# One step of a hybrid diffusion backbone: more weight parts made by transfers, and the attention placed anew

## The chip, the core and the metric

The kernel runs on one core of a Trainium2 chip. The metric is device time in microseconds (us) of one launch; lower is better. In the profile PE is TensorE, PEld its weight load, DVE VectorE, ACT ScalarE, POOL GpSimd, and SP the engine that issues most of the DMAs.

## The reference

One trunk layer, D = 2048, two request groups of 128 tokens each (context tokens and latent tokens), all in fp32:

```python
m = silu(c) @ w_ada + b_ada                       # shift, scale, gate, twice
h = rms_norm(x) * (1 + scale1) + shift1
qA, kA, vA, qB, kB, vB, gA, gB = split(h @ w_in)  # 2048 x 8704
oA = windowed GQA with sink, QK-norm, rotary      # 8 heads, 2 key heads, cached context
oB = 2-D neighbourhood attention with bias        # 8 heads, cached context
x  = x + gate1 * ((sigmoid(gA) * (oA @ w_br_a) + sigmoid(gB) * (oB @ w_br_b)) @ w_out)
h2 = rms_norm(x) * (1 + scale2) + shift2
x  = x + gate2 * (relu(h2 @ w_up) ** 2 @ w_down)  # 2048 x 8192 and back
```

The outputs are both groups' `x` and the new context keys and values.

## The kernel before

The weights are read once, in 456 steps of 128 x 1024 fp32 (512 KB). Steps 0 to 135 are `w_in` (the projections up to step 85, then the gates gB, gA), 136 to 167 the two branch projections, 168 to 199 `w_out`, and 200 to 455 the MLP: `w_up` in eight pieces p, with `w_down` interleaved.

TensorE multiplies in fp32r, which is narrower than fp32, so every weight is split in two: a high part `wH` (fp32r copy of the loaded `raw`, ScalarE, line 103) and a low part `wL` = `raw` - `wH` (VectorE, line 269). A product then takes three matmuls: high times high, low times high, high times low. A plain step has 12 matmuls of 128 x 512. In the pieces 1 to 7 of `w_up` some pairs of steps (`FAST`, by position) run a Strassen-like scheme instead: x (6 matmuls) and y (15), whose operands `XH`, `XL`, `YB`, `tH`, `tL`, `uH`, `uL` ScalarE and VectorE make (lines 1299 to 1325); slow pairs have 24.

Where the parts come from is set by three lists. A step in `LO_DMA` has its low part made by `minus_plus`: ScalarE writes -`wH` (line 275), and an accumulating DMA on GpSimd's queue adds the weight once more from memory (line 276). `XL_DMA` does the same for the `XL` of a fast pair (index 8 p + position). A step in `HI_DMA` has its high part loaded by a casting DMA on GpSimd's queue (line 239); if it is in `LO_DMA` as well, there is no `raw`, no copy and no subtraction. In the kernel before `HI_DMA` is empty.

All these tiles share one pool of 50 buffers. Each engine works its instructions off in the order in which the program emits them. That order is written out by hand in tables: `run()` walks the steps; `RUN[i]` tells how many steps ahead of step i (beyond `LOAD` = 4) the loads are emitted, `LOOK[i]` how many steps ahead the parts are made, and low parts by transfer two steps (`LO_AHEAD`) before that. `DOTS` places the dot products of the gate and modulation vectors (line 1476, VectorE, a tile each, one dot per request group) among the steps. `POST` gives for each projection unit the steps at which its squares are taken, its norm is applied, and it is transposed; `JOBS` the steps of the attention's stages.

VectorE also does the softmax reductions, ScalarE the squares (753), the norm's application (764), exponentials (866, 872), gates (671), and the evacuations of transposes (103, 800). TensorE transposes (794, 888) and multiplies (895).

Of the kernel before, what the change touches and what calls it, by code (L numbers as in the profile page):

```python
# [31 lines left out]
LOAD = 4  # L32
FB_DVE = 2
FB1 = 10
H_AT = 2
FILL = {1: [("gB", 2), ("gB", 3)], 3: [("gB", 0), ("gB", 1)]}
DOTS1 = [9, 11, 14, 19, 22, 24, 25, 27, 28, 30, 32, 33, 34, 35, 37, 40, 41, 42, 44, 46, 48, 49, 51, 53]
CHUNKS = [2, 2, 2, 4, 6]
NFAST = 8
FAST = {1: (0, 2, 5, 7), 2: (0, 4, 5, 6, 7), 3: (0, 2, 4, 5, 7), 4: (0, 2, 4, 5, 7), 5: (0, 1, 3, 4, 7), 6: (0, 3, 4, 5, 7), 7: (0, 1, 3, 6, 7)}  # L40
SEED_AT = 3
QK_ACT = [('qB', 1)]
H2_DVE = [(0, 1), (0, 3), (1, 1), (1, 3)]
KEEP = True
ROWS_AT = [8, 11, 7]
SEED1_AT = 2
SEED1 = "111110100100111111011111111011011111"
BACK = 9
AWAY = [('gA', 1), ('gB', 2), ('gB', 3), ('gA', 0), ('gB', 0), ('gA', 2)]
GATE_BACK = 2  # L50
DIRECT = (3,)
LO_DMA = [50, 54, 56, 63, 77, 107, 129, 141, 145, 176, 184, 188, 189, 203, 228, 233, 250, 286, 297, 360, 388, 392, 403, 447]
LO_AHEAD = 2

LOOK = "610013015100121312024402233324102425654224523344556654121016645555652437464478554443414661516353316110022636320000411134313543044023400458230315565645456443574337324421522555644666784051000205311111322534111433455554321045445111013410444324654734331001335565775443654453304436533423355423455542233213213545587654334232213213202440122544412433432313432443523324313211333435533333213331314344422557756822145342656433332302254541454475574464555546763333345544"
RUN = "345110004667224234111350007998421004464200022565595544354324444434399864356664356543323535443144230021224242014401314415432457530331035587986564665545676867644543555342013141147676676965699967265287998988511453877787785653022200123446553345324545104653232464345673321110102122521121211202355533232133432223443232410110000000011234344212022112531112752123301000112323643331133410100122454235566436675432012021222210010001154457832224556577677636445664422134"
CONST_AT = [83, 79]
XL_DMA = [8]
HI_DMA = []
ADA_AT = [None, 4, 13, 22, 25]  # L60
XS_AT = {1: 3, 2: 25, 3: 34}
POST = {('kvA', 0): [81, 83, 89], ('qA', 0): [84, 86, 92], ('qA', 1): [86, 88, 92], ('kB', 0): [90, 94, 98], ('qB', 0): [94, 98, 104], ('kB', 1): [98, 101, 103], ('qB', 1): [102, 105, 107]}
JOBS = [[93, 94, 95, 100, 106], [93, 94, 98, 104, 106], [98, 98, 100, 106, 114], [101, 104, 107, 110, 111], [107, 107, 110, 115, 120], [109, 109, 111, 118, 121], [113, 114, 115, 126, 128], [116, 116, 119, 122, 124]]
SS_AT = [120, 127]
T_AT = [4, 4]
PREP_IN = [5, 7]
DOTS = [44, 58, 61, 61, 62, 63, 65, 66, 66, 66, 69, 70, 71, 71, 72, 74, 76, 81, 84, 85, 89, 91, 94, 96, 96, 96, 100, 100, 101, 102, 102, 105, 107, 107, 107, 110, 110, 111, 113, 114, 115, 117, 117, 117, 120, 120, 120, 121, 121, 123, 123, 124, 127, 128, 128, 132, 132, 133, 133, 134, 135, 136, 141, 143, 144, 144, 149, 151, 151, 152, 157, 157, 157, 162, 163, 170, 172, 174, 174, 174, 176, 176, 178, 182, 183, 187, 190, 190]
# [13 lines left out]
def tile_hybrid_step(ctx: ExitStack, tc: tile.TileContext, a):  # L81
# [148 lines left out]
    def add_step(src, mm, key, half=0):  # L230
# [59 lines left out]

    by_dma = sorted(LO_DMA)

    def run():
        loads.sort(key=lambda x: x[:2])
        for st in wsteps:
            while loads and loads[0][0] <= st["i"] + int(RUN[st["i"]]):
                loads.pop(0)[2]()
            for j in sorted(j for j in pre if j <= st["i"]):
                for fn in pre.pop(j):
                    fn()  # L300
            to = st["i"] + int(LOOK[st["i"]]) + 1
            while by_dma and by_dma[0] < to + LO_AHEAD:
# [945 lines left out]
    def up_pair(p):  # L1248
        n0, n1 = PIECES[p]
        w, box, key = a["w_up"], {"begun": set()}, ("up", n0)  # L1250
        fast = FAST[p]

# [28 lines left out]
        for pos, is_fast in enumerate(kinds):  # L1281
# [90 lines left out]
            for i, (nm, pf, mf) in enumerate((("x", prep_x, mm_x), ("y", prep_y, mm_y))):  # L1372
# [284 lines left out]
```

## Time and profile before

| | |
|---|---|
| median of 3 runs | 1315.7 us (1315.65 to 1315.85) |
| the profiled execution | 1315.82 us |
| its span | 1314.0 us |
| TensorE busy | 1300.4 us, 99% |
| VectorE busy | 1147.5 us, 87% |
| ScalarE busy | 918.2 us, 70% |
| GpSimd busy | 61.3 us, 5% |
| HBM over the span | 291 GB/s |
| granted clock | 1.00 throughout (the upper of the two levels, 2.4 GHz) |

The span runs from the first instruction to the last; 1.8 us of the execution lie outside it. The shares of busy time are averages over stages with different limits, so the stages are read one by one in the rows further down.

### The profile page before, as it was taken

How to read it: one execution, taken by the hardware profiler on the slowest of the kernel's cores; microseconds unless marked ns; L12 is line 12 of the kernel's file. 1: busy time of each engine (PE TensorE's matmuls, PEld its weight loads, DVE VectorE, ACT ScalarE, POOL GpSimd, SP SyncE). 2: the span in 40 equal slices, each digit the busy share in tenths (PEclk: the TensorE clock that was granted, in tenths of full speed). 3: DMA queues.
4: the chain of work that ended last, by engine and by line, in shares of the span. 5: the costliest groups of instructions: out<-in, count | busy, mean ns of one | idle time of the engine just before them, and what ended most of it. 6: DMA issues, size and time to landing. Idle time of an engine off the chain costs nothing.

```text
span 1314.0 us, 17445 instructions
## 1 busy us (share of the span) xinstructions
PE 1300.4 (99%) x5978; PEld 1051.5 (80%) x5978; DVE 1147.5 (87%) x1531; ACT 918.2 (70%) x1299; POOL 61.3 (5%) x67
## 2 busy tenths in 40 slices
PE   8999999999999999999999999999999999999998
PEld 4677888888777788888888888888888888888886
DVE  4578999999899999999879998897989998979753
ACT  5656766689865655745687867869678687796881
POOL 0000000332100000000000000000000000000000
PEclk9999999999999999999999999999999999999999
DMA  9999999898889999999398775888586697867692
GB/s 373 408 406 410 378 362 323 317 325 296 287 344 388 401 387 315 372 356 375 107 335 300 261 250 173 279 292 280 199 299 230 211 317 250 295 160 304 197 349 80
DMA packets 148313, 393.80 MB, mean 300 GB/s; under 512 B 51680, under 2 KB 52672, under 8 KB 148224
## 3 DMA queue, kind: packets, MB, share of 16 engines
q1 hardware_dynamic: 144064, 378.18, 78.7%
q0 software_dynamic: 4016, 14.42, 5.7%
q8 instruction: 47, 0.77, 0.2%
q14 instruction: 42, 0.34, 0.1%
q10 hardware_dynamic: 144, 0.08, 0.0%
HBM read 373.97 MB, written 8.70 MB: 291 GB/s over the span
## 4 chain that ended last, share of the span: by engine, by line
PE 68%; DVE 4%; DMA 2%; ACT 2%; issue 1%; ACTq 0%; DVEq 0%; SPq 0%
PE acc L321 14%; PE acc L322 14%; PE acc L320 14%; PE Q L1259 6%; PE Q L1260 6%; PE Q L1258 6%; DVE aT L1476 1%; DVE wL L269 1%; DMA raw<-in_w_br_a 1%; DVE junk L1476 1%; DMA g_gA<-gm_gA 1%; PE Z L1259 1%; PE Z L1260 1%; PE Z L1258 1%; DMA gm_gA<-g_gA 1%
## 5 line engine op out<-in xcount | busy, mean ns | idle before, releaser
L269 DVE TENSOR_TENSOR wL<-raw,wH 128x1024 fp32r<-128x1024 f32 x361 | 425.8, 1224 | 63.6 <-ACT wH L103 62.8
L103 ACT ACTIVATE wH<-raw 128x1024 fp32r<-128x1024 f32 (+1 forms) x391 | 387.7, 1043 | 62.3 <-PE acc L321 9.6
L1476 DVE SCALAR_TENSOR_TENSOR aT<-aT,cB 128x1024 f32<-128x1024 f32 x144 | 173.9, 1224 | 1.1
L1476 DVE SCALAR_TENSOR_TENSOR junk<-aT,cB 128x1024 bf16<-128x1024 f32 x144 | 173.9, 1224 | 0.0
L451 PE MATMUL acc<-wH,hH 128*128 128x512 f32 x276 | 108.4, 393 | 0.7 <-ACT acc L103 0.7
L452 PE MATMUL acc<-wL,hH 128*128 128x512 f32 x276 | 107.5, 389 | 0.0
L453 PE MATMUL acc<-wH,hL 128*128 128x512 f32 x276 | 107.4, 389 | 0.0
L103 ACT ACTIVATE uH<-raw 128x1024 fp32r<-128x1024 f32 x34 | 36.1, 1063 | 65.4 <-DVE raw L1322 59.8
L451 PEld LDWEIGHTS acc<-wH,hH 128*128 128x128 f32 x276 | 51.8, 188 | 15.0 <-issue 2.5
L453 PEld LDWEIGHTS acc<-wH,hL 128*128 128x128 f32 x276 | 51.8, 188 | 11.0
L452 PEld LDWEIGHTS acc<-wL,hH 128*128 128x128 f32 x276 | 51.8, 188 | 10.4
L103 ACT ACTIVATE tH<-t 128x1024 fp32r<-128x1024 f32 x34 | 36.0, 1058 | 28.7 <-DVE t L1315 27.7
L320 PE MATMUL acc<-wH,hH 128*128 128x512 f32 x128 | 52.3, 408 | 0.0
L321 PE MATMUL acc<-wL,hH 128*128 128x512 f32 x128 | 50.2, 392 | 0.6 <-DVE wL L269 0.6
L486 PE MATMUL acc<-wH,hH 128*128 128x512 f32 x128 | 50.4, 393 | 0.0
L487 PE MATMUL acc<-wL,hH 128*128 128x512 f32 x128 | 50.0, 390 | 0.2 <-DVE wL L269 0.2
L322 PE MATMUL acc<-wH,hL 128*128 128x512 f32 x128 | 50.0, 391 | 0.0
L488 PE MATMUL acc<-wH,hL 128*128 128x512 f32 x128 | 49.9, 390 | 0.0
L1325 DVE TENSOR_TENSOR uL<-raw,uH 128x1024 fp32r<-128x1024 f32 x34 | 41.7, 1225 | 1.1
L1315 DVE TENSOR_TENSOR t<-raw 128x1024 f32<-128x1024 f32 x34 | 41.4, 1219 | 1.3 <-PE Q L1259 1.3
L1324 DVE TENSOR_TENSOR tL<-t,tH 128x1024 fp32r<-128x1024 f32 x34 | 41.4, 1219 | 0.0
L103 ACT ACTIVATE acc<-dsum 128x512 f32<-128x512 f32 x56 | 31.7, 589 | 13.8 <-DVE up L1360 7.1
(649 smaller groups left out, 3337.7 us busy)
## 6 DMA issues: line engine op xcount, KB each, us to landing
raw<-in_w_in SPq DMA_DIRECT2D x133, 512.0 KB, 8.0
raw<-in_w_down SPq DMA_DIRECT2D x128, 512.0 KB, 5.8
aT<-in_w_adaT SPq DMA_DIRECT2D x80, 512.0 KB, 8.3
raw<-in_w_upF SPq DMA_DIRECT2D x68, 512.0 KB, 5.5
aT<-in_w_gT SPq DMA_DIRECT2D x64, 512.0 KB, 6.8
raw<-in_w_up SPq DMA_DIRECT2D x60, 512.0 KB, 6.1
araw<-in_w_pair SPq DMA_DIRECT2D x48, 512.0 KB, 9.6
raw<-in_w_out SPq DMA_DIRECT2D x32, 512.0 KB, 10.0
```

Source lines behind the costliest of these rows:

```text
L103: act.activation(out, in_, AF.Copy)
L269: dve.tensor_tensor(st["lo"], st["raw"], st["hi"].bitcast(F32), op=OP.subtract)
L320: pe.matmul(acc[tb], sh, wh[:, k, :], start=f, stop=False, skip_group_check=seeded)
L321: pe.matmul(acc[tb], sh, wl[:, k, :], start=False, stop=False, skip_group_check=seeded)
L322: pe.matmul(acc[tb], sl, wh[:, k, :], start=False, stop=l, skip_group_check=seeded)
L451: pe.matmul(acc[tb], sh, wh[:, k, :], start=opened[u] and k == 0, stop=False, skip_group_check=skip)
L452: pe.matmul(acc[tb], sh, wl[:, k, :], start=False, stop=False, skip_group_check=skip)
L453: pe.matmul(acc[tb], sl, wh[:, k, :], start=False, stop=last and k == 1, skip_group_check=skip)
L1258: pe.matmul(acc, stat[0], hi, start=f, stop=False)
L1259: pe.matmul(acc, stat[0], lo, start=False, stop=False)
L1260: pe.matmul(acc, stat[1], hi, start=False, stop=l)
L1476: dve.scalar_tensor_tensor(out, box["raw"], 1.0, cB[s, tag], op0=OP.mult, op1=OP.mult, accum_out=dst[:, s, fb:fb + 1])
```

## The change

Only tables change. `HI_DMA` gets 26 steps of the MLP, 21 of which are in `LO_DMA` too, all of them new there; the other five (270, 272, 276, 336, 340) still load `raw`. In `LO_DMA` 144 stands for 141 as well. `XL_DMA` gets five fast pairs, of pieces 2 and 4, and in those two pieces `FAST` has other positions. `RUN` and `LOOK` change in 29 and 14 places, between steps 54 and 125; the attention's tables change by one to two steps; one `DOTS` entry goes from 61 to 58. Instruction counts stay on TensorE and ScalarE (26 copies to `wH` become 26 negating copies), VectorE has 26 subtractions fewer, GpSimd's queue 52 DMAs more, SP's 21 fewer.

```diff
-H_AT = 2
+H_AT = 3
...
-FAST = {1: (0, 2, 5, 7), 2: (0, 4, 5, 6, 7), 3: (0, 2, 4, 5, 7), 4: (0, 2, 4, 5, 7), 5: (0, 1, 3, 4, 7), 6: (0, 3, 4, 5, 7), 7: (0, 1, 3, 6, 7)}
+FAST = {1: (0, 2, 5, 7), 2: (0, 3, 4, 6, 7), 3: (0, 2, 4, 5, 7), 4: (0, 4, 5, 6, 7), 5: (0, 1, 3, 4, 7), 6: (0, 3, 4, 5, 7), 7: (0, 1, 3, 6, 7)}
...
-SEED1 = "111110100100111111011111111011011111"
+SEED1 = "111110100100111111011111111001011111"
...
-GATE_BACK = 2
+GATE_BACK = 1
...
-LO_DMA = [50, 54, 56, 63, 77, 107, 129, 141, 145, 176, 184, 188, 189, 203, 228, 233, 250, 286, 297, 360, 388, 392, 403, 447]
+LO_DMA = [50, 54, 56, 63, 77, 107, 129, 144, 145, 176, 184, 188, 189, 203, 223, 228, 233, 234, 237, 243, 250, 266, 286, 297, 306, 308, 341, 349, 357, 360, 373, 381, 388, 389, 392, 403, 425, 430, 436, 440, 442, 446, 447, 451, 453]
...
-XL_DMA = [8]
-HI_DMA = []
+XL_DMA = [8, 19, 20, 22, 36, 38]
+HI_DMA = [223, 234, 237, 243, 266, 270, 272, 276, 306, 308, 336, 340, 341, 349, 357, 373, 381, 389, 425, 430, 436, 440, 442, 446, 451, 453]
...
-POST = {('kvA', 0): [81, 83, 89], ('qA', 0): [84, 86, 92], ('qA', 1): [86, 88, 92], ('kB', 0): [90, 94, 98], ('qB', 0): [94, 98, 104], ('kB', 1): [98, 101, 103], ('qB', 1): [102, 105, 107]}
+POST = {('kvA', 0): [81, 83, 89], ('qA', 0): [84, 86, 92], ('qA', 1): [84, 86, 90], ('kB', 0): [88, 92, 96], ('qB', 0): [94, 98, 104], ('kB', 1): [98, 101, 103], ('qB', 1): [102, 106, 107]}
...
-SS_AT = [120, 127]
+SS_AT = [118, 127]
...
-STAT_AT = [-1, -1, 8, 15]
+STAT_AT = [-2, -1, 8, 17]
...
-M_AT = [6, 6, 9]
+M_AT = [4, 6, 9]
```

Of `JOBS` one normalisation goes from step 98 to 99, one transpose from 106 to 105.

The first place is GpSimd's queue from the first fast pair of the MLP on (piece 1 of `w_up`), before:

```order
L276 DMA XL<-in_w_upF 128x1024
L276 DMA wL<-in_w_up 128x1024
L276 DMA wL<-in_w_down 128x1024
L276 DMA wL<-in_w_up 128x1024 x2
L276 DMA wL<-in_w_down 128x1024 x2
L276 DMA wL<-in_w_up 128x1024
L276 DMA wL<-in_w_down 128x1024 x3
```

and now, up to the high part of step 276 (the rows before reach to the end of the kernel):

```order
L276 DMA XL<-in_w_upF 128x1024
L239 DMA wH<-in_w_up 128x1024
L276 DMA wL<-in_w_up 128x1024 x2
L239 DMA wH<-in_w_down 128x1024 x2
L276 DMA wL<-in_w_down 128x1024 x3
L239 DMA wH<-in_w_down 128x1024
L276 DMA wL<-in_w_down 128x1024
L276 DMA wL<-in_w_up 128x1024
L276 DMA XL<-in_w_upF 128x1024 x3
L239 DMA wH<-in_w_down 128x1024
L276 DMA wL<-in_w_down 128x1024
L239 DMA wH<-in_w_down 128x1024 x3
```

Casting loads (line 239) and accumulations (line 276) now alternate in one in-order queue.

The second is ScalarE's queue at piece 2 of `w_up`, steps 251 to 260, before:

```order
L103 ACTIVATE wH<-raw 128x1024 x5
L103 ACTIVATE XH<-raw 128x1024
L103 ACTIVATE YB<-raw 128x512
L103 ACTIVATE tH<-t_7225 128x1024
L103 ACTIVATE uH<-raw 128x1024
L103 ACTIVATE XH<-raw 128x1024
L103 ACTIVATE YB<-raw 128x512
L103 ACTIVATE tH<-t_7244 128x1024
L103 ACTIVATE uH<-raw 128x1024
L103 ACTIVATE XH<-raw 128x1024
```

and now:

```order
L103 ACTIVATE wH<-raw 128x1024 x3
L103 ACTIVATE XH<-raw 128x1024
L275 ACTIVATE XL<-XH 128x1024
L103 ACTIVATE YB<-raw 128x512
L103 ACTIVATE tH<-t_7189 128x1024
L103 ACTIVATE uH<-raw 128x1024
L103 ACTIVATE XH<-raw 128x1024
L275 ACTIVATE XL<-XH 128x1024
L103 ACTIVATE YB<-raw 128x512
L103 ACTIVATE tH<-t_7235 128x1024
L103 ACTIVATE uH<-raw 128x1024
L103 ACTIVATE wH<-raw 128x1024 x2
```

Steps 254 and 255 have become a fast pair; the second `XH` is that of step 256, which before was the first. Each of the two is followed by its negating copy.

The third is VectorE's queue at steps 56 to 62, where `junk` and `aT` are the two dots of a tile, before:

```order
L107 TENSOR_TENSOR hL_1828<-xnT_79,hH_1827 128x512
L269 TENSOR_TENSOR wL<-raw,wH 128x1024 x2
L1476 SCALAR_TENSOR_TENSOR junk,gc_g_361<-aT,cB_1115 128x1024
L269 TENSOR_TENSOR wL<-raw,wH 128x1024 x5
L1476 SCALAR_TENSOR_TENSOR aT,gc_g_361<-aT,cB_1117 128x1024
L269 TENSOR_TENSOR wL<-raw,wH 128x1024
L1476 SCALAR_TENSOR_TENSOR junk,gc_g_361<-aT,cB_1115 128x1024 x2
```

and now:

```order
L107 TENSOR_TENSOR hL_1830<-xnT_79,hH_1829 128x512
L269 TENSOR_TENSOR wL<-raw,wH 128x1024 x2
L1476 SCALAR_TENSOR_TENSOR junk,gc_g_361<-aT,cB_1115 128x1024 x2
L269 TENSOR_TENSOR wL<-raw,wH 128x1024 x5
L1476 SCALAR_TENSOR_TENSOR aT,gc_g_361<-aT,cB_1117 128x1024 x2
L269 TENSOR_TENSOR wL<-raw,wH 128x1024
L1476 SCALAR_TENSOR_TENSOR junk,gc_g_361<-aT,cB_1115 128x1024
```

One dot pair has moved ahead: its first dot stands before the five `wL` of steps 60 to 65 rather than behind them.

## Rows read from the trace of the kernel before

**Rows 1.** Windows: PE, PEld, DVE, ACT, POOL busy us (count), clock, DMA share, GB/s.

```profile
400.00:450.00 50.00, 49.97 (x266) 39.21 (x266) 49.97 (x79) 28.32 (x36) 0.86 (x1) 1.00 1.03 395
700.00:750.00 50.00, 50.00 (x222) 41.42 (x221) 48.75 (x62) 39.98 (x40) 0.86 (x1) 1.00 0.95 328
1200.00:1250.00 50.00, 50.00 (x223) 41.40 (x222) 38.43 (x40) 36.20 (x43) 0.00 (x0) 1.00 0.67 216
```

**Rows 2.** Waits of TensorE, 250 to 480 us: releaser, us in total, times, longest.

```profile
PE ps_PT L888 <- ACT T_qB L800: 0.9, 1, 0.9
PE acc L321 <- DVE wL L269: 0.8, 2, 0.6
PE ps_o L895 <- ACT probT L103: 0.8, 1, 0.8
PE acc L451 <- ACT acc L103: 0.7, 1, 0.7
PE ps_qT L794 <- ACT T_kB L103: 0.4, 1, 0.4
PE ps_qT L794 <- DVE oLA L904: 0.4, 1, 0.4
PE ps_gr L1497 <- DVE gc_g L1482: 0.2, 1, 0.2
```

**Rows 3.** Waits of VectorE, 204 to 475 us, the largest.

```profile
DVE wL L269 <- ACT wH L103: 3.6, 3, 2.8
```

**Rows 4.** Timeline, VectorE at step 61: start, duration, engine, line, instruction, [idle before].

```profile
203.64 1.23 DVE L269 TENSOR_TENSOR wL<-raw,wH 128x1024 fp32r<-128x1024 f32 x1 [0.25 <-ACT wH L103]
```

**Rows 5.** Timelines of ScalarE, TensorE and VectorE at five places of the attention.

```profile
259.32 1.06 ACT L103 ACTIVATE wH<-raw 128x1024 fp32r<-128x1024 f32 x1 [1.47 <-DVE aT L1476]
...
260.92 0.50 PE L451 MATMUL acc<-wH,hH 128*128 128x512 f32 x1 [0.70 <-ACT acc L103]
...
336.55 0.40 PE L321 MATMUL acc<-wL,hH 128*128 128x512 f32 x1
...
338.27 1.22 DVE L269 TENSOR_TENSOR wL<-raw,wH 128x1024 fp32r<-128x1024 f32 x1
...
347.36 1.23 DVE L269 TENSOR_TENSOR wL<-raw,wH 128x1024 fp32r<-128x1024 f32 x1 [2.85 <-ACT wH L103]
```

**Rows 6.** Accumulating DMAs: all; the one at 755.6; plain loads (KB, us to landing).

```profile
L276 POOL DMA_DIRECT2D wL<-in_w_down x6: 861/863/866, 708.7 to 1270.7; - x6
DMA to landing us min/median/max: 5.3/8.7/10.4
...
L276 POOL DMA_DIRECT2D wL<-in_w_up x1: 857/857/857, 755.6 to 755.6; - x1
DMA to landing us min/median/max: 5.3/5.3/5.3
...
raw<-in_w_down SPq DMA_DIRECT2D x128, 512.0 KB, 5.8
```

**Rows 7.** Timelines, first operand of the fast pair at step 256.

```profile
768.83 1.05 ACT L103 ACTIVATE XH<-raw 128x1024 fp32r<-128x1024 f32 x1
...
771.42 1.22 DVE L1315 TENSOR_TENSOR t<-raw 128x1024 f32<-128x1024 f32 x1
...
784.70 0.39 PE L1259 MATMUL Q<-XL,h20H 128*128 128x512 f32 x1
```

**Rows 8.** Timelines, step 389 and its neighbours.

```profile
1108.68 1.23 DVE L1325 TENSOR_TENSOR uL<-raw,uH 128x1024 fp32r<-128x1024 f32 x1
...
1117.09 1.04 ACT L103 ACTIVATE XH<-raw 128x1024 fp32r<-128x1024 f32 x1
...
1131.01 0.39 PE L1259 MATMUL Q<-wL,h23H 128*128 128x512 f32 x1
```

**Rows 9.** DMA queues: packets, MB, share of 16 engines' span.

```profile
q1 hardware_dynamic: 144064, 378.18, 78.7%
q0 software_dynamic: 4016, 14.42, 5.7%
```

More of the change, by code (lines that the diff above doesn't have):

```diff
@@ L53 @@
 LO_AHEAD = 2
-LOOK = "610013015100121312024402233324102425654224523344556654121016645555652437464478554443414661516353316110022636320000411134313543044023400458230315565645456443574337324421522555644666784051000205311111322534111433455554321045445111013410444324654734331001335565775443654453304436533423355423455542233213213545587654334232213213202440122544412433432313432443523324313211333435533333213331314344422557756822145342656433332302254541454475574464555546763333345544"
-RUN = "345110004667224234111350007998421004464200022565595544354324444434399864356664356543323535443144230021224242014401314415432457530331035587986564665545676867644543555342013141147676676965699967265287998988511453877787785653022200123446553345324545104653232464345673321110102122521121211202355533232133432223443232410110000000011234344212022112531112752123301000112323643331133410100122454235566436675432012021222210010001154457832224556577677636445664422134"
+LOOK = "610013015100121312024402233324102425654224523344556654121016645565652437574377445343414661516353205210022636320000411134313643044023400458230315565645456443574337324421522555644666784051000205311111322534111433455554321045445111013410444324654734331001335565775443654453304436533423355423455542233213213545587654334232213213202440122544412433432313432443523324313211333435533333213331314344422557756822145342656433332302254541454475574464555546763333345544"
@@ L57 @@
+RUN = "345110004667224234111350007998421004464200022565595544243214333434399864346555377654224635443144230021224242114401324405201346530331035587986564665545676867644543555342013141147676676965699967265287998988511453877787785653022200123446553345324545104653232464345673321110102122521121211202355533232133432223443232410110000000011234344212022112531112752123301000112323643331133410100122454235566436675432012021222210010001154457832224556577677636445664422134"
 CONST_AT = [83, 79]
-XL_DMA = [8]
@@ L59 @@
-HI_DMA = []
+XL_DMA = [8, 19, 20, 22, 36, 38]
+HI_DMA = [223, 234, 237, 243, 266, 270, 272, 276, 306, 308, 336, 340, 341, 349, 357, 373, 381, 389, 425, 430, 436, 440, 442, 446, 451, 453]
 ADA_AT = [None, 4, 13, 22, 25]
 XS_AT = {1: 3, 2: 25, 3: 34}
-POST = {('kvA', 0): [81, 83, 89], ('qA', 0): [84, 86, 92], ('qA', 1): [86, 88, 92], ('kB', 0): [90, 94, 98], ('qB', 0): [94, 98, 104], ('kB', 1): [98, 101, 103], ('qB', 1): [102, 105, 107]}
-JOBS = [[93, 94, 95, 100, 106], [93, 94, 98, 104, 106], [98, 98, 100, 106, 114], [101, 104, 107, 110, 111], [107, 107, 110, 115, 120], [109, 109, 111, 118, 121], [113, 114, 115, 126, 128], [116, 116, 119, 122, 124]]
@@ L64 @@
-SS_AT = [120, 127]
+POST = {('kvA', 0): [81, 83, 89], ('qA', 0): [84, 86, 92], ('qA', 1): [84, 86, 90], ('kB', 0): [88, 92, 96], ('qB', 0): [94, 98, 104], ('kB', 1): [98, 101, 103], ('qB', 1): [102, 106, 107]}
+JOBS = [[93, 94, 95, 100, 106], [93, 94, 99, 104, 106], [98, 98, 100, 105, 114], [101, 104, 107, 110, 111], [107, 107, 110, 115, 120], [109, 109, 111, 118, 121], [113, 114, 115, 126, 128], [116, 116, 119, 122, 124]]
+SS_AT = [118, 127]
 T_AT = [4, 4]
 PREP_IN = [5, 7]
-DOTS = [44, 58, 61, 61, 62, 63, 65, 66, 66, 66, 69, 70, 71, 71, 72, 74, 76, 81, 84, 85, 89, 91, 94, 96, 96, 96, 100, 100, 101, 102, 102, 105, 107, 107, 107, 110, 110, 111, 113, 114, 115, 117, 117, 117, 120, 120, 120, 121, 121, 123, 123, 124, 127, 128, 128, 132, 132, 133, 133, 134, 135, 136, 141, 143, 144, 144, 149, 151, 151, 152, 157, 157, 157, 162, 163, 170, 172, 174, 174, 174, 176, 176, 178, 182, 183, 187, 190, 190]
+DOTS = [44, 58, 58, 61, 62, 63, 65, 66, 66, 66, 69, 70, 71, 71, 72, 74, 76, 81, 84, 85, 89, 91, 94, 96, 96, 96, 100, 100, 101, 102, 102, 105, 107, 107, 107, 110, 110, 111, 113, 114, 115, 117, 117, 117, 120, 120, 120, 121, 121, 123, 123, 124, 127, 128, 128, 132, 132, 133, 133, 134, 135, 136, 141, 143, 144, 144, 149, 151, 151, 152, 157, 157, 157, 162, 163, 170, 172, 174, 174, 174, 176, 176, 178, 182, 183, 187, 190, 190]
```

## The prediction

> **What bounds the kernel now.** I read the table of windows first, since a busy share over the whole span says little. From 700 us on every 50 us window holds 50.00 us of TensorE work in 222 or 223 matmuls at the full clock, so one matmul is retired every 0.226 us; VectorE meanwhile sinks to 38.43 us in one window [rows 1]. In the MLP TensorE is thus saturated, and nothing that VectorE is spared there can shorten it. The second view is the waits. Between 250 and 480 us TensorE loses time to seven releasers, 4.2 us by the view's sums [rows 2]; after 480 us the same view lists none. The third is who sets those waits. In 400 to 450 us VectorE is busy 49.97 of 50 us [rows 1]; in all of 204 to 475 us its largest releaser is ScalarE's `wH`, 3.6 us in three waits, 2.85 of them at 347.36 [rows 3, 5]. There VectorE, with ScalarE's chain ahead of 346 us, sets the pace, and TensorE meets it at each wait. The end is VectorE's time at about 475 us plus some 838 us of TensorE without a wait.
>
> So three questions decide: does VectorE reach 475 us earlier; does a TensorE wait survive that VectorE doesn't then absorb; and does a tile of the MLP now come late.
>
> **The front, up to 250 us.** One dot pair moves from step 61 to 58. On VectorE this puts a second `junk` dot ahead of five `wL` instructions. At 203.64 us VectorE idled 0.25 us until ScalarE had made `wH` of step 61 [rows 4]. A dot of 1.22 us now stands ahead of the same instruction, so that idle time is filled: -0.25 us, which VectorE carries to the end of the attention. Its operand must be there; it is loaded ten steps ahead, and the dots that it joins waited for nothing. `H_AT` 3 is the maximum with 53, and the seed that `SEED1` drops is written anyway: nothing.
>
> **The attention.** `wH` of step 85 moves to an earlier group; at 259.32 ScalarE stood in it and held the seed of the accumulator that follows, and TensorE waited 0.70 us until 260.92 [rows 5]. This wait should go. It gains nothing at the end, since VectorE's order of work after it isn't shortened, and TensorE meets the next VectorE or ScalarE wait that much sooner.
> The pair `wH`, `wL` of step 104 moves from the group of step 97 to that of step 102. There `wL` stands behind eight more dots and two applies. By the row at 338.27, which is step 105's `wL` and starts when step 102's three dots are done, with one `wL` (1.14 from start to start) taken out ahead of it, step 104's would start near 337.1 and end near 338.3; TensorE wants it at 336.55 [rows 5]. A new wait of about 1.7 us. Behind it on TensorE stand eleven matmuls and the transposes of `u_qB`, which before waited for `T_kB` 0.4 and then for `T_qB` 0.9 us [rows 2]. These two take up 1.3 of the 1.7; the rest, 0.4, falls to the two waits after them (`oLA` 0.4, `probT` 0.8 [rows 2]). VectorE's next reductions wait for none of it. Net 0; bounds -0.7 (the first wait's gain stays) and +0.6.
> `qA` group 1 and `kB` group 0 move two steps forward. Their applies, squares and transposes are the same instructions on both engines and stand before and after the same anchors, so ScalarE's unbroken stretch of work holds as much as before up to the `wH` that VectorE awaits at 347.36 [rows 5]. Net 0.
> Step 144 makes its low part by a transfer in place of 141: one subtraction against another, both ahead of the gate sum that TensorE awaits at 475 us (`gc_g`, 0.2 [rows 2]). `SS_AT`, `GATE_BACK`, `STAT_AT` and `M_AT` reorder what is between waits. Together 0, bounds -1.0 and +1.0: a quarter of the 4.2 us of waits either way.
>
> **The MLP.** Twenty-six subtractions of 1.22 us leave VectorE (31.7 us), 26 copies leave ScalarE and 26 negating copies replace them. TensorE gets no earlier from that: 222 matmuls per 50 us before and after [rows 1]. What can cost is lateness. A transferred low part runs: high part there, negation 1.06, 0.3 to the issue, then 5.3 to 10.4 us to landing, median 8.7 [rows 6]. A casting load isn't in the trace; bounds are the plain load's median of 5.8 us and the accumulating transfer's largest, 10.4 [rows 6]; I take 6 to 9, since it reads once and adds nothing.
> The two tightest places that I found:
> - The first operand of the third fast pair (step 256). The steps ahead of it were plain ones, and are now a fast pair, behind whose `uH` its `XH` stands on ScalarE. Before, `XH` ran at 768.83, `t` at 771.42 and VectorE's `XL` some 2.3 us after that, for use at 784.70 [rows 7]. Now two `wL` fewer (2.3) stand ahead of the first `t`, which starts near 769.1; its `YB` and two half-size sums (0.6 each) bring that pair's `uH` near 772.3, `XH` at 773.3, the negation at 774.2, the issue at 775.6. Landing 780.9 to 786.0, median 784.3; use, with the fast pair ahead taking 21 matmuls in place of 24, at 784.0. Wait 0 to 2.0, by the median 0.3. The transfer issued at 755.6, the nearest in time, took 5.3 us [rows 6], so I take 0.
> - Step 389. Its casting load needs the buffer that the `uL` of 1108.68 frees when it ends [rows 8], about 1.1 earlier now. Issued at 1109, it lands by 1115 to 1119.5. Its negation is placed behind `XH` (1117.09) and ahead of `YB`; TensorE uses the low part at 1131.01 [rows 8]. With 1119.2 for the issue it lands by 1129.6 at the longest: 0. Only a load beyond 9 us stalls ScalarE, and with it `YB`.
> Counted the same way, the others come out with 1 to 8 us in hand. I take 0 for the MLP, with bounds 0 and +5: 2.0 here, and 3 for loads that stall ScalarE at one or two of 26 places.
> The software queue's transfers keep the rings busier: 5.7% for 14.42 MB against 78.7% for 378.18 MB, 1.9 times the time per byte [rows 9]. Fifty-two more of them, 27 MB of writes, less 21 plain loads, add some 6 (casts at the plain price) to 8.5% of the span's ring time, all of it after 660 us. The plain loads may come later by some of it; I take 0 for it too, and its bound lies in that +5.
>
> VectorE runs two-input subtractions nearly all the time, and the issue on GpSimd's queue takes 861 to 866 ns in the MLP all the same [rows 6]. The Trainium skill (SBUF — State Buffer, in "SBUF: two separate sides") warns that software descriptors cannot be written while VectorE holds both read ports, and gives 620 ns alone against 3100 ns overlapped for a transfer. By its figures each of the 52 would be some 2.5 us later, step 256's wait about 2.5 and the sum near 1320; by the row nothing changes. The steady issue time speaks for the row.
>
> **The sum.** The profiled execution took 1315.82 us, 1.8 outside its span, and 0.1 above the median shown. -0.25 - 0 + 0 gives 1315.6, by the median 1315.4.
>
> **Rivals.**
> (a) Nothing that a measurement tells (0.2%, 2.6 us): 1315.4, own range 1313.5 to 1317.5. For it: saturation from 480 us, the unchanged VectorE work before 475 us.
> (b) Late tiles in the MLP: one mechanism, the casting load that lands later than 9 us after its issue, with other loads on its rings, and stalls ScalarE in its in-order queue at the negation, so that the copies behind come late as well. TensorE has no slack, so each adds in full: 1 to 3 us at two to four places, 1319, up to 1323. Against it: none of the transferred low parts of before is among TensorE's releasers [rows 2], and the counted places hold at the median landing.
> (c) The attention's waits go: TensorE's 4.2 us and VectorE's 2.85 us idle are the most that is there; if ScalarE reaches the `wH` of 347.36 the whole 2.85 us earlier and VectorE keeps that to 475 us, 1312.5. For it: `kB` group 0 leaves the crowded stretch in part. Against it: ScalarE's work ahead of that `wH` is the same.
> (d) GpSimd's issues are held until VectorE's instruction ends, one or two of its 1.22 us each time: every transfer 1.2 to 2.4 later, step 256 waits 1.5 to 2.7 and two to four others 1 each, 1320. Against it: the even issue times [rows 6]. This is what the skill's rule above would make of it.
>
> **Chances.** (a) 0.53, (b) 0.20, (c) 0.22, (d) 0.05. Faster by over 0.2%: most of (c), 0.20. Slower by over 0.2%: (b) and (d) mostly, 0.24. Within: 0.56. The range that leaves out 2 in 10: 1311.8 to 1319.8.
>
> **What would show it.** Right: no idle time on VectorE near 203.6; no TensorE wait at 260.9; a wait near 336.5 to 338 for `wL` and less at 339.7 and 341.8; no TensorE wait over 0.3 us after 640. Wrong: a TensorE wait after 640 us for a `wL` or `XL` that GpSimd's queue wrote, or for a `YB` behind a negation; accumulations that land later than 10.4 us; or VectorE reaching `gc_g` before 474.

## Result and profile after

| | before | after |
|---|---|---|
| median | 1315.9 us (1315.4 to 1316.0, 16 runs) | 1320.3 us (1316.9 to 1328.5, 16 runs) |
| ratio, 95% interval | | 1.0036, 1.0024 to 1.0047 |
| the profiled execution | 1315.82 us | 1328.52 us |
| its span | 1314.0 us | 1326.7 us |

The kernel became slower by 4.4 us, outside the range given, and its runs spread over 12 us where those of before spread over 0.6. The execution that was profiled is the longest of the 16; it shows four places where time can go, and other executions need not lose at all of them. What they cost in the median is taken from the experiments. One of the 12 executions of experiment 5 took 2678 us, for which there is no explanation; its ratio leaves that one out.

The page after, part 1 (busy us, share of the span, instructions) and the queues (packets, MB, share of 16 engines' span), which answer to [rows 9]:

```profile
PE 1304.1 (98%) x5978; PEld 1053.4 (79%) x5978; DVE 1119.9 (84%) x1505; ACT 920.0 (69%) x1299; POOL 97.5 (7%) x119
...
q1 hardware_dynamic: 141040, 367.17, 76.4%
q0 software_dynamic: 11504, 41.69, 14.5%
```

VectorE has 27.6 us less work (31.7 had been counted), and TensorE ends 12.7 us later in this execution. The software queue takes 8.8% of the rings more than before and the hardware queue 2.3% less; the difference of 6.5 lies in the 6 to 8.5 that had been estimated for it.

The attention after, by the waits of TensorE from 250 to 480 us, beside [rows 2]:

```profile
PE acc L321 <- DVE wL L269: 2.0, 3, 1.0
PE ps_o L895 <- ACT probT L103: 1.1, 1, 1.1
...
PE ps_PT L888 <- ACT T_qB L800: 0.3, 1, 0.3
...
PE ps_gr L1497 <- DVE gc_g L1482: 0.2, 1, 0.2
```

The wait for the seed of `acc` (0.7) is gone, the waits for `wL` have grown from 0.8 to 2.0, and `T_qB` has shrunk from 0.9 to 0.3: what was forecast. VectorE at step 61, TensorE at step 104 and VectorE ahead of the gate sum (timelines: start, duration, engine, line, instruction, idle time before), beside [rows 4, 5]:

```profile
203.34 5.76 DVE L269 TENSOR_TENSOR wL<-raw,wH 128x1024 fp32r<-128x1024 f32 x5
...
337.76 0.50 PE L321 MATMUL acc<-wL,hH 128*128 128x512 f32 x1 [1.04 <-DVE wL L269]
...
474.96 0.19 DVE L1482 TENSOR_TENSOR gc_g<-gc_g,cols 128x32 f32<-128x32 f32 x1
```

The five `wL` run without a pause where 0.25 us had been idle, and the attention ends a little earlier than before. The loss lies behind it. The waits of TensorE from 480 us on, of which before had none:

```profile
PE Q L1258 <- ACT dsum L103: 4.7, 2, 2.7
PE acc L321 <- DMA wL<-in_w_down: 2.1, 1, 2.1
PE acc L320 <- ACT acc L103: 1.7, 1, 1.7
```

The windows show where (PE, PEld, DVE, ACT, POOL busy us with counts; granted clock; DMA share; GB/s):

```profile
740.00:745.00 5.00, 5.00 (x24) 4.14 (x23) 3.90 (x6) 4.17 (x4) 0.00 (x0) 1.00 1.28 84
745.00:750.00 5.00, 4.75 (x21) 3.59 (x20) 4.44 (x4) 3.38 (x4) 0.00 (x0) 1.00 1.09 86
750.00:765.00 15.00, 13.16 (x58) 10.89 (x59) 7.05 (x9) 9.08 (x8) 0.87 (x1) 1.00 0.87 330
765.00:770.00 5.00, 3.04 (x11) 2.13 (x10) 4.96 (x7) 4.10 (x7) 0.00 (x0) 0.88 1.03 274
770.00:775.00 5.00, 5.00 (x19) 4.00 (x18) 4.96 (x7) 4.26 (x5) 0.86 (x1) 0.78 0.73 299
...
925.00:930.00 5.00, 3.34 (x15) 2.46 (x14) 3.09 (x4) 4.97 (x6) 0.00 (x0) 1.00 0.94 380
1105.00:1110.00 5.00, 2.57 (x12) 1.79 (x10) 2.72 (x3) 4.97 (x5) 0.00 (x0) 1.00 0.92 354
1110.00:1115.00 5.00, 4.69 (x14) 3.76 (x15) 3.55 (x5) 5.00 (x7) 0.85 (x1) 0.66 0.45 105
```

and of before, the first two:

```profile
740.00:745.00 5.00, 5.00 (x23) 4.14 (x23) 5.00 (x8) 3.74 (x4) 0.00 (x0) 1.00 0.95 332
745.00:750.00 5.00, 5.00 (x23) 4.13 (x22) 5.00 (x6) 5.00 (x5) 0.00 (x0) 1.00 0.85 308
```

Between 740 and 750 us the rings (the queues of the core's 16 DMA engines) are busier than before and move about a quarter of the bytes. TensorE's gaps beyond its pace of 0.227 us are 2.25 us at 749, 2.12 at 765, 1.82 at 926 and 2.90 at 1107; after the second and the last the granted clock is down (0.78 and 0.66), which makes matmuls start every 0.43 us for a while and costs 1.7 and 1.6. With 0.26 at 1299 that is 12.65; less the 0.44 us by which TensorE passes the gate sum earlier (475.30 against 475.74) it is 12.2 of the 12.7 between the spans. The gap at 749 is the low part of step 243 itself, written by GpSimd's queue (the second line of the waits above); those at 765, 926 and 1107 come by way of ScalarE.

What runs at 740 us shows in the DMA view of 733 to 744 us (queues as above; issues with KB and us to landing):

```profile
DMA packets 4045, 1.97 MB, mean 179 GB/s; under 512 B 3799, under 2 KB 3799, under 8 KB 4044
...
q1 hardware_dynamic: 3996, 1.77, 85.0%
q0 software_dynamic: 48, 0.18, 26.5%
...
wL<-in_w_down POOLq DMA_DIRECT2D x1, 512.0 KB, 14.7
raw<-in_w_down SPq DMA_DIRECT2D x1, 512.0 KB, 13.5
aT<-in_w_gT SPq DMA_DIRECT2D x1, 512.0 KB, 12.8
raw<-in_w_upF SPq DMA_DIRECT2D x1, 512.0 KB, 13.4
pTa<-pla SPq DMA_TRANSPOSE x2, 10.2
```

Two transposing DMAs (`flip`, line 964: the relu-squared activations, planes `pla` to `pTa`) send, by their size, the 3799 small packets, and the accumulating transfer of step 243, issued 0.06 us after the second, shares the rings with them. In this stretch its packets take 26.5% of 16 engines for 11.0 us over 48 of them, 0.97 us each; over the span of before they took 0.30 ([rows 9]: 5.7% of 16 times 1314.0 us over 4016). The second transposing DMA lands after 14.9 us and the accumulation after 14.7; three plain loads behind them land after 13 us, where the median of before was 5.8 [rows 6].

ScalarE after, at this place (timeline):

```profile
752.05 2.53 ACT L103 ACTIVATE fTa<-pTa 128x2048 uint16<-128x2048 uint16 x1 [3.68 <-DMA pTa<-pla]
...
759.13 1.06 ACT L103 ACTIVATE wH<-raw 128x1024 fp32r<-128x1024 f32 x1 [2.51 <-DMA raw<-in_w_up]
...
766.86 2.04 ACT L103 ACTIVATE dsum<-acc 128x512 f32<-128x512 f32 x4
```

and before:

```profile
748.71 2.52 ACT L103 ACTIVATE fTa<-pTa 128x2048 uint16<-128x2048 uint16 x1
...
760.91 1.07 ACT L103 ACTIVATE dsum<-acc 128x512 f32<-128x512 f32 x2
762.91 1.28 ACT L103 ACTIVATE dsum<-acc 128x512 f32<-128x512 f32 x2 [0.93 <-PE acc L322]
```

Two waits for landings, 6.2 us together, stand ahead of the evacuation `dsum` in ScalarE's queue. It starts 5.95 us later than before, of which TensorE's own delay up to here is 1.8 (2.25 less 0.44), and TensorE can't start the next sum before it.

The second of the two loads wasn't slow itself: it landed 6.6 us after its issue. SyncE issued it late, at 752.41 where it had been 743.75 before, because its own in-order queue stood waiting for the second transposing DMA to land. SyncE's waits from 730 to 770 us have the line

```profile
SPq L243 <- DMA pTa<-pla: 8.8, 1, 8.8
```

which the same view of before doesn't have. So a late transfer delays others in two ways: those in flight beside it, and those that SyncE can't issue until it lands.

At 926 us ScalarE stands in waits of the same kind; ScalarE after:

```profile
919.66 1.06 ACT L103 ACTIVATE wH<-raw 128x1024 fp32r<-128x1024 f32 x1 [0.35 <-DMA raw<-in_w_down]
922.59 1.06 ACT L103 ACTIVATE wH<-raw 128x1024 fp32r<-128x1024 f32 x1 [1.87 <-DMA raw<-in_w_down]
...
927.08 1.10 ACT L103 ACTIVATE acc<-dsum 128x512 f32<-128x512 f32 x2
```

Plain loads of steps 309 and 310, issued behind transfers of steps 306 and 308 and two transposing DMAs, hold the copies 2.2 us, and behind them the seed of `acc` that TensorE awaits. The landing of all 16 transposing DMAs (min, median, max), after and then before:

```profile
DMA to landing us min/median/max: 4.3/7.5/14.9
```

```profile
DMA to landing us min/median/max: 4.2/4.6/8.5
```

### The profile page after: what moved, and what is told of

The parts are those of the page before. It is cut to its first block, busy times and chain, and to the rows that moved or that the text cites. A ratio compares the mean times of both kernels' runs of the same rounds, so it can differ in the third digit from the quotient of the medians.

```text
span 1326.7 us, 17547 instructions
## 1 busy us (share of the span) xinstructions
PE 1304.1 (98%) x5978; PEld 1053.4 (79%) x5978; DVE 1119.9 (84%) x1505; ACT 920.0 (69%) x1299; POOL 97.5 (7%) x119
## 4 chain that ended last, share of the span: by engine, by line
PE 60%; DMA 7%; issue 4%; DVE 4%; ACT 3%; POOL 0%; SPq 0%; ACTq 0%; POOLq 0%; DVEq 0%
PE acc L321 11%; PE acc L320 11%; PE acc L322 11%; PE Q L1258 6%; PE Q L1259 6%; PE Q L1260 6%; DMA aT<-in_w_gT 2%; DVE wL L269 1%; DMA wL<-in_w_down 1%; DMA aT<-in_w_adaT 1%; DVE aT L1476 1%; DMA wH<-in_w_down 1%; ACT wH L103 1%; DVE junk L1476 1%; DMA raw<-in_w_br_a 1%
## 5 line engine op out<-in xcount | busy, mean ns | idle before, releaser
L269 DVE TENSOR_TENSOR wL<-raw,wH 128x1024 fp32r<-128x1024 f32 x340 | 402.6, 1223 | 91.1 <-ACT wH L103 84.4
L103 ACT ACTIVATE wH<-raw 128x1024 fp32r<-128x1024 f32 (+1 forms) x365 | 364.6, 1044 | 72.9 <-DMA raw<-in_w_down 13.8
L452 PEld LDWEIGHTS acc<-wL,hH 128*128 128x128 f32 x276 | 51.8, 188 | 10.4
L275 ACT ACTIVATE wL<-wH 128x1024 fp32r<-128x1024 f32 x45 | 47.6, 1058 | 13.5 <-DMA wH<-in_w_down 11.3
L103 ACT ACTIVATE fTa<-pTa 128x2048 uint16<-128x2048 uint16 x16 | 40.5, 2529 | 3.7 <-DMA pTa<-pla 3.7
```

Of the source, the lines that this page charges most:

```text
L103: act.activation(out, in_, AF.Copy)
L269: dve.tensor_tensor(st["lo"], st["raw"], st["hi"].bitcast(F32), op=OP.subtract)
L452: pe.matmul(acc[tb], sh, wl[:, k, :], start=False, stop=False, skip_group_check=skip)
```

## Experiments

The theories: that the new accumulating transfers load the rings, so that loads and transposing DMAs land late (the rings); that the negating copies, 26 instructions in ScalarE's in-order queue, some of which wait for casting loads, hold it (ScalarE's queue); that the attention tables lose the time. Diffs are against the changed kernel; lines left out are marked, among them those of `LO_DMA` and `FAST` where the words above the diff tell them. Each run has runs of the kernel before beside it (medians 1315.8 to 1315.9).

**1. The attention tables alone**, the MLP's lists as before.

```diff
-XL_DMA = [8, 19, 20, 22, 36, 38]
-HI_DMA = [223, 234, 237, 243, 266, 270, 272, 276, 306, 308, 336, 340, 341, 349, 357, 373, 381, 389, 425, 430, 436, 440, 442, 446, 451, 453]
+XL_DMA = [8]
+HI_DMA = []
...
```

> The attention tables of the changed kernel, the MLP lists (high parts by casting loads, low parts by accumulating transfers, XL by transfer, places of the fast pairs) of the kernel before. Theory A, the loss is made in the MLP by transfers that land late: 1315.2 to 1316.2, and no TensorE wait after 640 us over 0.3 us. Theory B, a part of the loss comes from the attention or from the state in which it leaves the queues: 1317 or more.

Measured: 1315.6 us, ratio 0.9999 (0.999 to 1.0007). The attention is out.

**2. The MLP's lists alone**, the attention's tables as before.

```diff
-H_AT = 3
+H_AT = 2
...
-STAT_AT = [-2, -1, 8, 17]
+STAT_AT = [-1, -1, 8, 15]
...
```

> The converse: MLP lists of the changed kernel, attention tables of the kernel before. Theory A: 1318 to 1323 and a wide spread from run to run, as for the whole change, with TensorE waits of 2 us after 700 us. Theory B: under 1317.5.

Measured: 1319.0 us, 1.0032 (1.0018 to 1.0046). The loss is made in the MLP.

**3. No casting loads**: all low parts as in the changed kernel, high parts by ScalarE.

```diff
-HI_DMA = [223, 234, 237, 243, 266, 270, 272, 276, 306, 308, 336, 340, 341, 349, 357, 373, 381, 389, 425, 430, 436, 440, 442, 446, 451, 453]
+HI_DMA = []
```

> The changed kernel without its 26 casting loads (26 more copies on ScalarE and 21 more plain loads on SP); its accumulating transfers stay. Theory A1, it is the casting loads that land late and stall ScalarE at the negation behind them: 1315.3 to 1316.5. Theory A2, it is the accumulating transfers and the ring time of all the added bytes together: 1318 to 1322.

Measured: 1331.0 us, 1.0116 (1.0102 to 1.0129), much slower than either theory had. Its windows, 650 to 1300 us:

```profile
650.00:1300.00 650.00, 640.40 (x2810) 525.85 (x2808) 518.62 (x593) 511.40 (x567) 31.24 (x36) 1.00 0.86 273
```

ScalarE is busy 511.4 us there, against 491.0 before and 487.8 after, and most of TensorE's waits are for it (`acc` 5.9, `dsum` 1.7). Without the casting loads ScalarE has 26 copies more and can't keep up, so here they pay for the negations. Whether they have a part in the loss this run can't tell, since it adds a larger loss of another kind; 4 and 5, which keep them, tell it.

**4. Casting loads, but the low parts by subtraction** as before.

```diff
-XL_DMA = [8, 19, 20, 22, 36, 38]
+XL_DMA = [8]
...
```

> The changed kernel with its 26 casting loads, but the low parts in the MLP made as before (26 subtractions back on VectorE, every raw loaded). Theory A1 with ScalarE's stall at the negation as the link: 1315.5 to 1317, since no negation waits for a cast. Theory A2: 1317 to 1320, the rings still carry 26 transfers more.

Measured: 1316.5 us, 1.0006 (0.9997 to 1.0015), with one wait of TensorE after 480 us, of 0.3 us. The casting loads by themselves cost 0.7 us, which isn't clear of the interval. Yet the transposing DMAs have a median landing of 7.3 us here, against 4.6 before, 7.5 after, and 4.9 in experiment 3, which has the accumulations and no casting loads. So it is with the casting loads that the median comes later, and that costs little; the longest landing is 9.2 us here and 14.9 after.

**5. Casting loads and negating copies, but not the 26 new accumulating transfers**, so that those low parts hold only the negated high part.

```diff
-    def minus_plus(lo, hi, src):
+    def minus_plus(lo, hi, src, add=True):
...
-        pool.dma_start(lo, src.bitcast(F32R), accum_op=OP.add)
+        if add:
+            pool.dma_start(lo, src.bitcast(F32R), accum_op=OP.add)
...
-        minus_plus(st["lo"], st["hi"], st["src"])
+        minus_plus(st["lo"], st["hi"], st["src"], st["i"] not in NEW_LO)
...
```

> The changed kernel with its casting loads and its 26 new negating copies, in the same order, but without the 26 accumulating transfers behind them (the weight isn't added to the negated high part: those low parts are wrong). Theory R, the transfers cost by landing late and by holding the rings, so that plain loads land late too: 1315.7 to 1317, ScalarE's waits for landings back to under 15 us after 640 us (25 to 35 before). Theory S, it is ScalarE's in-order queue, in which the negating copies and the earlier places of the high parts push back what TensorE waits for: 1318 to 1322.

Measured: 1315.6 us, 0.9999 (0.999 to 1.0007), TensorE without a wait after 480 us.

```profile
650.00:1300.00 650.00, 650.00 (x2868) 537.54 (x2867) 530.43 (x607) 492.29 (x549) 23.74 (x37) 1.00 0.79 261
```

This tells the rings from ScalarE's queue: the same instructions on ScalarE and VectorE, the same casting loads, and without the accumulations nothing is lost. It doesn't tell how much an accumulation costs by being late itself and how much by what it delays, for both go with it. The DMA share falls from 0.90 (the changed kernel, same window) to 0.79.

**6. As 5, also without the casting loads.**

```diff
-HI_DMA = [223, 234, 237, 243, 266, 270, 272, 276, 306, 308, 336, 340, 341, 349, 357, 373, 381, 389, 425, 430, 436, 440, 442, 446, 451, 453]
+HI_DMA = []
...
```

> The same without the casting loads: only 26 more negating copies on ScalarE, 26 subtractions fewer on VectorE, the order of the run without casts (which took 1331), no ring traffic added. Theory R: 1315.5 to 1318. Theory S: 1325 to 1332, since ScalarE's work (511 of 650 us after 650) and its order are what they were there.

Measured: 1328.0 us, 1.0091 (1.0078 to 1.0104), ScalarE busy 515.7 of 650 us. That is the range of the theory of ScalarE's queue: the negations do hold ScalarE where no casting load stands in for the copies, which isn't the case in the changed kernel. Whether it is ScalarE's time or the buffers that the `raw` tiles keep was not separated.

**7. Loads one step earlier** from step 215 on (`RUN` plus one), to give late landings more room.

```diff
-RUN = "345110004667224234111350007998421004464200022565595544243214333434399864346555377654224635443144230021224242114401324405201346530331035587986564665545676867644543555342013141147676676965699967265287998988511453877787785653022200123446553345324545104653232464345673321110102122521121211202355533232133432223443232410110000000011234344212022112531112752123301000112323643331133410100122454235566436675432012021222210010001154457832224556577677636445664422134"
+RUN = "345110004667224234111350007998421004464200022565595544243214333434399864346555377654224635443144230021224242114401324405201346530331035587986564665545676867644543555342013141147676676965699967265287998988511453877788896764133311234557664456435656215764343575456784432221213233632232322313466644343244543334554343521221111111122345455323133223642223863234412111223434754442244521211233565346677547786543123132333321121112265568943335667688788747556775533245"
```

> The changed kernel with every load of the steps from 215 on emitted one step (2.72 us) earlier. Theory R, in the form that landing took 1 to 2 us longer and the lead is short: 1315.7 to 1318. If the loads are held by the 50 buffers rather than by their place in the order, or under theory S: 1318 to 1322, unchanged.

Measured: 1334.6 us, 1.015 (1.0128 to 1.0173), worse than either range. Two transposing DMAs took 15.1 and 17.6 us and two accumulations came 2.2 and 4.2 us late at TensorE. Earlier loads gave no room here; whether the fuller rings or the 50 buffers are the reason was not separated.

**8. The fast pairs and `XL_DMA` as before**, all else changed.

```diff
-XL_DMA = [8, 19, 20, 22, 36, 38]
+XL_DMA = [8]
...
```

> The changed kernel with the places of the fast pairs and the one XL transfer of the kernel before; its casting loads and 21 new low parts by transfer stay. If the moved pairs and their five XL transfers make a good part of the loss: 1316 to 1317.5. If the 21 low parts do: 1318.5 to 1322.

Measured: 1319.3 us, 1.0033 (1.002 to 1.0046), with waits at the same places (749, 765, 925 us). The loss is there without the moved fast pairs and their five operands; the 1.0 us between the medians lies within the spread of the runs.

**9. Only step 243 by transfers**, on the quiet kernel of experiment 1.

```diff
...
-HI_DMA = [223, 234, 237, 243, 266, 270, 272, 276, 306, 308, 336, 340, 341, 349, 357, 373, 381, 389, 425, 430, 436, 440, 442, 446, 451, 453]
+HI_DMA = [243]
```

> The kernel with the new attention and the MLP lists of before (1315.6), plus one changed step: 243 loads its high part by a casting transfer and makes its low part by an accumulating one. Theory C, an accumulating transfer that is issued while the transposing transfers of the pieces are in flight holds all rings (in the changed kernel both took 14.7 and 14.9 us near 737 us, at 84 GB/s, and the loads behind them 13): this one step brings a part of the loss by itself, a TensorE wait of 1 to 3 us near 750 us, 1317 to 1320. Theory L, it is the sum of the added load on the rings: 1315.5 to 1316.0, no such wait.

Measured: 1315.3 us, 0.9997 (0.9988 to 1.0005). One such pair of transfers at the worst place costs nothing by itself: there the accumulation was issued 1.11 us after the transposing DMA, and they took 8.3 and 7.5 us.

**10. All but 243.**

```diff
-HI_DMA = [223, 234, 237, 243, 266, 270, 272, 276, 306, 308, 336, 340, 341, 349, 357, 373, 381, 389, 425, 430, 436, 440, 442, 446, 451, 453]
+HI_DMA = [223, 234, 237, 266, 270, 272, 276, 306, 308, 336, 340, 341, 349, 357, 373, 381, 389, 425, 430, 436, 440, 442, 446, 451, 453]
...
```

> The changed kernel with step 243 as before (plain load, copy, subtraction), the other 20 new low parts stay. Theory C: the waits at 750 and 765 us and the slow matmuls after them go, about half of the loss: 1317 to 1318.5. Theory L: 1319.5 to 1321.

Measured: 1318.8 us, 1.0028 (1.0016 to 1.004), between the two ranges. In its trace the waits at 749 and 765 us are gone, and waits of 0.4 us at 836 and 1.4 at 921 are left.

**11. All but 243, 306 and 308.**

```diff
-HI_DMA = [223, 234, 237, 243, 266, 270, 272, 276, 306, 308, 336, 340, 341, 349, 357, 373, 381, 389, 425, 430, 436, 440, 442, 446, 451, 453]
+HI_DMA = [223, 234, 237, 266, 270, 272, 276, 336, 340, 341, 349, 357, 373, 381, 389, 425, 430, 436, 440, 442, 446, 451, 453]
...
```

> The changed kernel without 243, 306 and 308, whose transfers stood beside transposing ones near 737 and 901 to 910 us. Theory C: 1316 to 1317.3, the waits at 750, 765 and 925 us gone. Theory L: 1319 to 1320.5.

Measured: 1316.3 us, 1.0005 (0.9996 to 1.0014), and TensorE without a wait in the MLP in its profiled execution:

```profile
650.00:1300.00 650.00, 650.00 (x2868) 537.58 (x2867) 532.42 (x609) 492.63 (x549) 42.16 (x57) 1.00 0.88 279
```

Three steps of 26 carry 4.0 of the 4.4 us. The DMA share is still 0.88, so it isn't the mean load that costs, but these transfers at their places.

**12. The three moved to 246, 309 and 311** rather than taken out.

```diff
-HI_DMA = [223, 234, 237, 243, 266, 270, 272, 276, 306, 308, 336, 340, 341, 349, 357, 373, 381, 389, 425, 430, 436, 440, 442, 446, 451, 453]
+HI_DMA = [223, 234, 237, 246, 266, 270, 272, 276, 309, 311, 336, 340, 341, 349, 357, 373, 381, 389, 425, 430, 436, 440, 442, 446, 451, 453]
...
```

> The changed kernel with the same number of transfers, but those of the steps 243, 306 and 308 at 246, 309 and 311, so that their accumulations are issued some 8 us later, behind the transposing transfers. Theory C: 1316 to 1318. Theory L (the load is the same): 1319.5 to 1321.5.

Measured: 1325.5 us, 1.0073 (1.006 to 1.0087), outside both ranges. The loss at 243 is gone, but ScalarE's and then TensorE's timeline show another, and the windows behind it (columns as above) a clock that fell to its lower level (0.50, 1.2 GHz):

```profile
920.75 1.06 ACT L275 ACTIVATE wL<-wH 128x1024 fp32r<-128x1024 f32 x1 [4.95 <-DMA wH<-in_w_down]
...
926.77 0.79 PE L320 MATMUL acc<-wH,a4H 128*128 128x512 f32 x1 [7.01 <-ACT acc L103]
```

```profile
925.00:930.00 5.00, 3.23 (x8) 2.56 (x9) 3.75 (x7) 4.74 (x7) 0.00 (x0) 0.50 0.34 66
930.00:935.00 5.00, 5.00 (x22) 4.08 (x21) 5.00 (x6) 3.17 (x4) 0.00 (x0) 0.92 0.02 3
```

A casting load took 10.4 us to land and stalled ScalarE at the negation; the copies, and the seed behind them, came late. That is rival (b)'s mechanism, here in one place 7.0 us and some 2 of slow clock. So moving these transfers off the transposing DMAs didn't remove the loss, but put another in its place.

**13. Only the three** on the quiet kernel, **14. 243 moved to 246** alone, and **15. all but 306 and 308.**

```diff
-HI_DMA = [223, 234, 237, 243, 266, 270, 272, 276, 306, 308, 336, 340, 341, 349, 357, 373, 381, 389, 425, 430, 436, 440, 442, 446, 451, 453]
+HI_DMA = [243, 306, 308]
...
+HI_DMA = [223, 234, 237, 246, 266, 270, 272, 276, 306, 308, 336, 340, 341, 349, 357, 373, 381, 389, 425, 430, 436, 440, 442, 446, 451, 453]
...
+HI_DMA = [223, 234, 237, 243, 266, 270, 272, 276, 336, 340, 341, 349, 357, 373, 381, 389, 425, 430, 436, 440, 442, 446, 451, 453]
```

> The new attention, the MLP lists of before, plus the three steps 243, 306 and 308 with casting and accumulating transfers. If these three bring the loss by themselves: 1318 to 1320. If they do so only beside the other 23 (the rings fuller, ScalarE and the queue differently timed), as the run with 243 alone suggests: 1315.3 to 1316.3.

> The changed kernel with 243's two transfers at step 246 instead, nothing else moved. If the loss at 750 and 765 us is the meeting of its accumulation with the transposing transfer: as without it, 1318 to 1319, no TensorE wait between 740 and 770 us. If it is one more transfer pair there: 1319.5 to 1321.

> The changed kernel without 306 and 308; 243 stays. The losses at 243 and at 306/308 are separate: 1317.3 to 1319, the waits at 750 and 765 us there and that at 925 gone. If they are tied together: 1316.3, as without the three.

Measured: 1317.2 us, 1.0014 (1.0006 to 1.0023); 1318.4 us, 1.0024 (1.0016 to 1.0033); 1318.3 us, 1.0024 (1.0011 to 1.0037). TensorE's waits from 480 us on, in 13:

```profile
PE acc L320 <- ACT acc L103: 1.4, 1, 1.4
```

and in 15, where the accumulation of step 243 took 11.0 us and TensorE didn't wait for it:

```profile
PE Q L1258 <- ACT dsum L103: 1.2, 1, 1.2
PE acc L320 <- ACT acc L103: 0.3, 1, 0.3
```

The first lies between its two ranges, the other two in those of separate losses. Steps 306 and 308 cost 1.4 us with no other new transfers about but 243's, which cost nothing alone (9). Step 243 costs only where the others are there too: 2.0 us in 15 against 11. Moving its transfers three steps on (14) leaves no wait between 740 and 770 us in its trace, which is of its shortest execution, and takes as long as leaving them out (10: 1318.8). The two places look separate: next to 11, which lacks all three, 306 and 308 cost 2.5 us (10) and 243 costs 2.0 (15). Against the changed kernel itself only the 4.0 us of 11 is clear; the 1.5 and 1.9 of 10 and 15 lie within the spread of its runs.

No version is faster than the kernel before: 1 and 9 are equal to it within their intervals.

## Why the prediction was wrong

**Right: what bounds the kernel.** TensorE in the MLP gains nothing from an idle VectorE. Experiment 5 leaves VectorE 530.43 us of work in place of 558.21 between 650 and 1300 us, and takes the time of before.

**Right: the front and the attention.** The idle time at 203.64 is filled, `gc_g` is written 0.44 us earlier (0.20 in experiment 1, 0.25 said), the wait at 260.9 is gone, the new one at step 104 is 1.04 us (1.7 said) and is taken up by those behind it. Experiment 1 gives 1315.6, the 1315.4 of the forecast within its interval.

**Right in itself: the counted places.** The operand of step 256 landed at 787.37 for a use at 789.88, and no instruction waited for the casting load of step 389, which landed after 3.8 us. The median landing of the accumulations is 8.5 us (8.7 taken), of the casting loads 8.1 (6 to 9 taken). Lines 239 and 276 (issue; landing min, median, max):

```profile
L239 POOL DMA_DIRECT2D wH<-in_w_down x21: 530/557/902, 699.3 to 1286.1; - x21
...
DMA to landing us min/median/max: 3.7/8.1/12.2
...
L276 POOL DMA_DIRECT2D wL<-in_w_down x22: 847/867/889, 708.3 to 1299.8; - x22
...
DMA to landing us min/median/max: 5.2/8.5/14.7
```

The issue of an accumulation takes 847 to 889 ns, where it was 861 to 866 in [rows 6], so rival (d) is out. Of the longer descriptor writing that the Trainium skill (SBUF — State Buffer, "SBUF: two separate sides") warns of, this trace shows nothing. The page says it of a VectorE instruction in a 2-port performance mode; for one with two SBUF inputs, such as these subtractions, it names only a GpSimd instruction that reads SBUF, so the prediction had taken its rule too widely.

**Wrong: the two zeros of the MLP, "I take 0 for the MLP" for the tiles that GpSimd's queue writes, and "The plain loads may come later by some of it; I take 0 for it too".** Together they measure +4.4 us, inside their bound of +5, which the range didn't reach. How the 4.4 of the median divides between them is not shown; in the profiled execution the first is 2.25 us at 749 and the second 2.12, 1.82 and 2.90, with the slow clock behind two of these.

The first failed at step 243, one of the others that were said to have "1 to 8 us in hand": its accumulation took 14.7 us, outside the 5.3 to 10.4 that [rows 6] gave as bounds. The second failed because the added ring time, estimated well, was taken as spread over the stretch from 660 us on, where the mean DMA share of before was 0.77. It matters where it falls: beside the transposing DMAs. In the kernel before, SyncE's queue, which carries them and the plain loads, took 97.5% of the rings from 733 to 744 us already, with 4216 of 4675 packets under 512 B. The transposing DMAs stood in no step of the prediction. The tiles that were delayed there, `pTa` and plain `raw`, had not been counted, though ScalarE's queue holds the evacuations and seeds that TensorE needs right behind them, nor had the loads that SyncE can't issue meanwhile. Of the signs of being wrong that the prediction named, two came: TensorE waited for a `wL` of GpSimd's queue, and accumulations landed later than 10.4 us.

**Rivals.** (b) named the time (1319, up to 1323) and the in-order queue of ScalarE, but another cause. In the changed kernel negations wait 11.3 us for casting loads in four places, and TensorE loses 0.26 us by it; what stalls ScalarE where it costs is `pTa` and `raw`. Experiment 12 alone shows (b) as it was written. Its chance of 0.20 was low for what the prediction knew: it rested on the median landing at the places counted, and no place had been counted for the loads that share the rings. That its time is near the measured one is luck as far as the changed kernel goes.

**Open.** Why steps 306 and 308 cost a steady 1.4 us and the loss at 243 varies with the run; where the long executions lose their time that have no transfers at 243 (up to 1326.0 us in 10, 1322.2 in 14), of which no trace was kept; which of the accumulation and the transposing DMA holds the other; the 0.4 us that are left without the three; and the place at 1107 us, where the wait was seen in the one long execution only (behind transposing DMAs of 10.6 and 12.5 us beside a casting load).

## What to carry to other kernels

A transfer that replaces an engine's instruction can be paid for by the transfers beside it, so look at the stretch where it will run, and at what else is on the rings there, transposing DMAs of small packets above all, not at the mean DMA share. Then follow the delayed tiles, not just the new ones, to each queue that works in order, the one that issues loads included: what it holds back may be a seed or an evacuation that the saturated engine waits for. Where one engine is saturated without a wait, as TensorE in this MLP, work taken off another gained nothing, and what was moved onto the rings could only cost.

## What was not expected of the hardware

- An accumulating transfer issued right behind a transposing DMA landed late, and the DMA with it. At step 243 with 0.04, 0.06 and 0.12 us between the two issues (experiment 8, after, experiment 15) it took 14.3, 14.7 and 11.0 us, and the DMA 14.6, 14.9 and 11.1; in five other kernels, with over 1 us between them (in two of these the accumulation was the earlier), 6.0 to 8.6 and the nearer of the two DMAs 6.3 to 7.5. In all eight it is the same transfer; the distance was not varied by itself, so this is a pattern, not shown as a cause.
- A TensorE wait of 2 to 3 us can be followed by a lower clock: 0.78 in 770 to 775 us after a wait of 1.96 us, and 0.66 in 1110 to 1115 after one of 2.74, with 1.7 and 1.6 us lost on top. After waits of 2.09 and 1.66 us the windows show 1.00, and so they do in experiment 8 after one of 2.8 us at 765. So the length of the wait alone doesn't decide it, and what does is open.
- Packets of the software queue took 0.97 us of ring time each beside the transposing DMAs of 733 to 744 us, and 0.30 in the mean of before.
